# Depthwise convolution taps split between ScalarE and VectorE, and six adaLN jobs issued earlier, in a two-layer hybrid decoder trunk

## The chip, the cores and the metric

The kernel runs on one core of one Trainium2 chip. The metric is the device time of one execution in microseconds, as the median over runs. In this text PE is TensorE (PEld its weight loads), DVE is VectorE, ACT is ScalarE, POOL is GpSimd and SP is SyncE, whose queue issues the DMAs.

## What is computed

```python
D_MODEL, SEQ, DEPTH, D_FF = 2048, 256, 2, 5632
CONV_CH, CONV_WIDTH = 512, 31            # the depthwise convolution of this case
IN_COLS = SB_COLS + CONV_COLS + NSA_COLS + MLA_COLS   # 1536 + 1024 + 1304 + 672

def conformer_conv(u, dw_w, dw_b, ln_g, ln_b, pw_w, pw_b):
    a, g = jnp.split(u, 2, axis=-1)
    h = causal_dwconv(a * jax.nn.sigmoid(g), dw_w, dw_b)     # 31 taps per channel
    ...                                                       # LayerNorm over the channels
    return jax.nn.silu(h) @ pw_w + pw_b

def hybrid_mixer(h, w_in, ...):
    u = h @ w_in
    u_sb, u_conv, u_nsa, u_mla = jnp.split(u, [OFF_CONV, OFF_NSA, OFF_MLA], axis=-1)
    o_sb = stick_breaking_attention(...)   # 8 heads
    o_conv = conformer_conv(u_conv, ...)
    o_nsa = nsa_attention(...)             # compressed, selected and window branches
    o_mla = mla_attention(u_mla, ...)      # low-rank q and kv latents
    y = concat([o_sb, o_conv, o_nsa, o_mla])
    y = rms_norm(y.reshape(B, T, 4, 512), group_norm.reshape(4, 512))
    return y.reshape(B, T, 2048) @ w_o

def conv_glu_ffn(h, w_up, conv_w, conv_b, w_down):
    u = causal_dwconv(h @ w_up, conv_w, conv_b)               # 3 taps
    a, g = jnp.split(u, 2, axis=-1)
    return (jax.nn.silu(g) * a) @ w_down

def reference(x, c, ada_w, ada_b, ...):
    cond = jax.nn.silu(c)
    for l in range(DEPTH):
        mod = cond @ ada_w[l] + ada_b[l]                      # adaLN: 2048 x 12288 weights a layer
        sh1, sc1, g1, sh2, sc2, g2 = jnp.split(mod, 6)
        h = rms_norm(x, norm_mix[l]) * (1 + sc1) + sh1
        x = x + g1 * hybrid_mixer(h, ...)
        h = rms_norm(x, norm_ffn[l]) * (1 + sc2) + sh2
        x = x + g2 * conv_glu_ffn(h, ...)
    return x
```

## The kernel before

**Stages.** Each of the two layers has a mixing part (input projection, the four head groups MLA, NSA, stick-breaking and convolution, then w_o) and an FFN (w_up, activation, w_down). The 256 tokens lie along the free dimension for most tiles (128 channels by 256 tokens). All weights come once from HBM, in chunks of at most 128x1024 in fp32. `load_w` loads such a chunk into one of four buffers of the tag `raw`. For most matmuls it then makes two fp32r parts of it: ACT casts `hi` (L247), DVE subtracts to get `lo` (L249), each in a ring of three. With `whole=True`, as the input projection of layer 0 does, PE multiplies the fp32 chunk itself.

**Order.** Each engine runs its instructions in one fixed order, which a list scheduler writes out when the kernel is built, from priorities and data dependences. All loads go through SP's one queue, in that order too: a load whose buffer is not free yet holds up the loads behind it.

**adaLN jobs.** The modulation vectors of the gates and of the FFN are made on DVE. A job of `ada_jobs` loads two chunks `adaw` (512 KB each, ring of three, L163) and runs one dot product with the conditioning vector on each (L167). Layer 0 needs 16 jobs for the mixing gate, then 32 for the FFN's shift and scale, then 16 for its gate. `tick` issues jobs: each `load_w` adds `rate[0]` to a credit, and a whole credit issues a job. The dots of a job run at the next job, or right behind a `lo` (L249). `rate[0]` is 0 throughout layer 0's input projection, and is set by `phase` afterwards (table RATE). `mod` issues at once whatever is still missing when a vector is used. For layer 0's FFN, `norm_chunk` uses `mod` in that way.

**The input projection of layer 0** (`mix_in_behind`) loads wconv and wlq beside the adaLN chunks of the first norm, and then calls `nsa_kv`, which loads 16 chunks wnkv (412 KB) and runs 128 matmuls (L322) on them. In layer 1 `nsa_kv` comes later, behind the taps.

**The taps.** `conv_glu` writes the gated signal `ug` (128 x 4 x 286 with its left padding). `conv_taps` then makes for each of 31 taps and each of the four 128-channel tiles one DVE instruction on 128x256: the first tap as a TENSOR_SCALAR with the bias (L617), the other 30 as a SCALAR_TENSOR_TENSOR, times a per-channel weight plus `acc` (L621). That is 124 per layer. The weights lie in the tile `vec`, one DMA per layer, which holds all small vectors. The taps are written with a priority that is lowered by DW_LATE = 800, so that they fill gaps. `conv_ln` needs them all. It is written behind the MLA group and the first stick-breaking gemm (`sb_gemm(l, 0)`).

**Tag sq4.** Pool `mr` has one buffer of 128x1024 with the tag `sq4`. It serves in turn `cv` (the projection's copy), the scratch of the squares in `group_norm_n` (L522, here the norm of MLA's output `om`), a tile of the NSA group, and the scratch of `conv_ln` and of later norms.

Of the kernel before, what the change touches and what calls it, by code (L numbers as in the profile page):

```python
# [11 lines left out]
F32 = mybir.dt.float32  # L12
F32R = mybir.dt.float32r
BF16 = mybir.dt.bfloat16
AF = mybir.ActivationFunctionType
ALU = mybir.AluOpType
# [4 lines left out]
P = 128  # L21
T = 256
# [7 lines left out]
CW = 31  # L30
# [32 lines left out]
RATE = ((0.45, 0.9, 0.45), (0.2, 0.8, 0.45))  # L63

RATE_FFN = ((0.16, 0.36), (0.12, 0.12))
ADA_LATE = ((2500, 2500, 300, 1500, 1500), (2500, 1000, 300, 2500, 2500))
GATE = ((1, 0, 0, 1, 1), (1, 0, 0, 1, 1))
DW_LATE = 800
# [7 lines left out]
def tile_trunk(ctx: ExitStack, tc: tile.TileContext, io, out, L):  # L76
    nc = tc.nc
# [64 lines left out]
    def vec(l, name):  # L142
        o, w = VEC[name]
        if o >= NVEC:
            if (l, 1) not in vecs:
                vecs[l, 1] = cp.tile([P, NVECS], F32, name=f"vs{l}")
                nc.sync.dma_start(vecs[l, 1], io["vecs"][l])
            return vecs[l, 1][:, o - NVEC:o - NVEC + w]
        if (l, 0) not in vecs:
            vecs[l, 0] = cp.tile([P, NVEC], F32, tag="vec", name="vec", bufs=1)  # L150
            nc.sync.dma_start(vecs[l, 0], io["vec"][l])
        return vecs[l, 0][:, o:o + w]
# [19 lines left out]
    def ada_dot(l, s, j, raw):  # L172
        for hf in range(2):
            ada_mul(ada_load(l, s, j, hf), s, j, hf, raw)
# [43 lines left out]
    def phase(l, i):  # L218
# [3 lines left out]
        gate[0] = GATE[l][i]  # L222
        late[0] = ADA_LATE[l][i]

# [10 lines left out]
    rate = [0.0]  # L235
# [23 lines left out]
    def products(w, act, weights_stand):  # L259

        hi, lo = w
        if lo is None:
            return [(hi, act)]
        x, xl = act[:, 0, :], act[:, 1, :]
        return [(hi, x), (hi, xl), (lo, x)] if weights_stand else [(hi, x), (lo, x), (hi, xl)]
# [68 lines left out]
    def act_whole():  # L334
        return actp.tile([P, 4, T], F32, tag="act", name="actw", bufs=12)
# [12 lines left out]
    def norm_stats(x, sp, pp, tag):  # L348

        ss = pp.tile([P, 2, T], F32, tag=tag, name="ss")  # L350
        acc = sp.tile([P, 4, T], F32, name="nacc")
        for c in range(4):
            xc = x[:, 4 * c:4 * c + 4, :]
            if c == 0:
                nc.scalar.activation(acc, xc, AF.Square)
                continue
            sq = sp.tile([P, 4, T], F32, tag="nsq4", name="sq", bufs=2)
            nc.scalar.activation(sq, xc, AF.Square)
            nc.vector.tensor_add(acc, acc, sq)
        nc.vector.tensor_add(acc[:, 0:2, :], acc[:, 0:2, :], acc[:, 2:4, :])  # L360
        for c in range(2):
            nc.tensor.matmul(ss[:, 0, :], ones, acc[:, c, :], start=(c == 0), stop=(c == 1))
        r = sp.tile([P, T], F32, tag="nr", name="r", bufs=1)
        rsqrt(r, ss[:, 0, :], D)
        return r
# [25 lines left out]
    def norm_chunk(dst, xc, r, a, sh, sp):  # L391

        t1 = sp.tile([P, T], F32, tag="nsq", name="t1", bufs=2)
        nc.vector.scalar_tensor_tensor(t1, xc, a, r, op0=ALU.mult, op1=ALU.mult)
        if is_whole(dst):
            nc.scalar.activation(dst, t1, AF.Identity, bias=sh)  # L396
            return
        nc.scalar.activation(dst[:, 0, :], t1, AF.Identity, bias=sh)
        nc.vector.scalar_tensor_tensor(  # L399
            dst[:, 1, :], t1, sh, dst[:, 0, :].bitcast(F32), op0=ALU.add, op1=ALU.subtract  # L400
        )

    def norm_hs():
        hs = []
        for _ in range(KD // 2):
            ht = act_pair()
            hs += [ht[:, 0], ht[:, 1]]
        return hs
# [12 lines left out]
    def mm_n(outs, w, h, first, last):  # L421

        prods = products(w, h, False)
        for tt in range(2):
            for i, (ww, xx) in enumerate(prods):
                for o, c0, c1, f in outs(tt):
                    nc.tensor.matmul(
                        o, xx[:, tt * P:(tt + 1) * P], ww[:, c0:c1],
                        start=(first and i == 0 and f), stop=(last and i == len(prods) - 1),
                        skip_group_check=True,  # L430
                    )
# [19 lines left out]
    def mix_in_behind(l, x, sp, pp, mr, conv):  # L451

        r = norm_stats(x, sp, pp, "gp")
        a = cp.tile([P, KD], F32, tag="amul", name="amul", bufs=2)
        g, ab = vec(l, "norm_mix"), vec(l, "ada_b")
        sh = cp.tile([P, KD], F32, name="sh0")
        sc = cp.tile([P, KD], F32, name="sc0")
        raws = [cp.tile([P, 2, KD], F32, name=f"raw0_{i}") for i in range(2)]
        hs, hw = norm_hs(), []
        for _ in range(KD // 4):  # L460
            t = act_whole()
            hw += [t[:, i, :] for i in range(4)]
        ps = [pp.tile([P, 2, T], F32, tag="gp", name="gt") for _ in range(4)]
        px = [pp.tile([P, 2, T], F32, tag="gx", name="gt") for _ in range(4)]
        for k in range(KD):
            for s, m in ((1, sc), (0, sh)):
                if s == 0:
                    w = load_w(io["wconv"][l, k], True)
                ada_dot(l, s, k, raws[s])
                nc.vector.scalar_tensor_tensor(  # L470
                    m[:, k:k + 1], raws[s][:, 0, k:k + 1], ab[:, s * KD + k:s * KD + k + 1],
                    raws[s][:, 1, k:k + 1], op0=ALU.add, op1=ALU.add,
                )
            nc.vector.scalar_tensor_tensor(
                a[:, k:k + 1], sc[:, k:k + 1], 1.0, g[:, k:k + 1], op0=ALU.add, op1=ALU.mult
            )
            norm_chunk(hw[k], x[:, k, :], r, a[:, k:k + 1], sh[:, k:k + 1], sp)
            split_chunk(hs[k], hw[k])
            mm_t(px, w, hw[k], 8, k == 0, k == KD - 1)
            if k == KD - 1:  # L480
                cv = [mr.tile([P, 4, T], F32, tag=t, name="cv") for t in ("sq4", "acc")]
                cv = [t[:, 2 * i:2 * i + 2, :] for t in cv for i in range(2)]
                for i in range(4):
                    nc.scalar.copy(cv[i], px[i])
                conv(cv)
            w = load_w(io["wlq"][l, k], True)
            mm_t(ps, w, hw[k], 5, k == 0, k == KD - 1)
            mm_n(lambda tt: [(ps[3][:, tt, :], 640, 896, tt == 0)], w, hw[k], k == 0, k == KD - 1)
        return hs, ps, nsa_kv(l, hw, mr, pp, "gx")

    def split_chunk(dst, src):
# [115 lines left out]
        return ug  # L607

    def conv_taps(l, ug, mp):
        acc = mp.tile([P, 4, T], F32, tag="acc", name="acc")  # L610
        dw = vec(l, "dw_w")
        db = vec(l, "dw_b")
        for j in range(CW - 1, -1, -1):
            for c in range(4):
                w = dw[:, c * CW + j:c * CW + j + 1]
                if j == CW - 1:
                    nc.vector.tensor_scalar(  # L617
                        acc[:, c, :], ug[:, c, j:j + T], w, db[:, c:c + 1], op0=ALU.mult, op1=ALU.add
                    )
                else:  # L620
                    nc.vector.scalar_tensor_tensor(  # L621
                        acc[:, c, :], ug[:, c, j:j + T], w, acc[:, c, :], op0=ALU.mult, op1=ALU.add
                    )
                yield acc

    def conv_ln(l, acc, mp, pp):
# [163 lines left out]
    def nsa_kv(l, h, mp, pp, tag="gp"):  # L790
        nkv = mp.tile([P, 2, 824], F32, name="nkv")
        ps = [[pp.tile([P, 2, T], F32, tag=tag, name="pn").rearrange("p a b -> p (a b)")[:, 0:412]
               for _ in range(2)] for _ in range(2)]
        gemm_n([io["wnkv"][l, k] for k in range(KD)], h, 824,
               lambda tt: [(ps[tt][s], s * 412, s * 412 + 412, True) for s in range(2)])
        for tt in range(2):
            for s in range(2):
                nc.scalar.copy(nkv[:, tt, s * 412:s * 412 + 412], ps[tt][s])
        return nkv
# [250 lines left out]
    for l in range(L):  # L1050
# [7 lines left out]
        with ExitStack() as s1:  # L1058
            p8 = _Tagged(pool(s1, f"p8_{l}", space=PSUM), {"gp": 4, "gx": 4})
            with ExitStack() as s0:  # L1060
                ug = []
# [5 lines left out]
                if l:  # L1067
                    h, ps = mix_in(l, x, r, sp, p8, conv)
                else:
                    h, ps, nkv = mix_in_behind(l, x, sp, p8, mr, conv)  # L1070
# [41 lines left out]
        for mg in range(2):  # L1112
            ps = gemm_t(pp, [io["wo"][l, mg, k] for k in range(KD)], y, 8)
            for m in range(8):
                c = mg * 8 + m
# [10 lines left out]
        with ExitStack() as s2:  # L1126
# [3 lines left out]
            h = norm_hs()  # L1130
# [10 lines left out]
            def up(g):  # L1141
                rate[0] = RATE_FFN[l][0] if g else 0.0
                ps = [pp.tile([P, 2, T], F32, tag="gp", name="gt") for _ in range(4)]
# [26 lines left out]
            def down(k0, acts, st=None):  # L1170
                rate[0] = RATE_FFN[l][1]
                for mg in range(4):
# [179 lines left out]
```

## Time and profile before

| | |
|---|---|
| median of 3 runs | 2453.43 us (2445.65 to 2476.61) |
| the profiled execution, its own time | 2452.41 us |
| span of that execution in the trace | 2450.6 us |
| PE busy | 2369.3 us (97%) |
| DVE busy | 1937.6 us (79%) |
| ACT busy | 1225.8 us (50%) |
| DMA moved | 609.82 MB, 249 GB/s over the span |

The span runs from the first to the last instruction in the trace, and the profiled execution is 1.8 us longer than it. A busy share is an average over stages with different limits, so the rows below are taken by stage. In layer 0, 165 to 209 us is `nsa_kv`. From 209 to 314 us run MLA, the first stick-breaking gemm and the preparation of NSA, up to the first use of the NSA scores (L951). The rest of the mixing part and w_o run from 314 us to 535 us, and the FFN begins there. In layer 1 the stretch from 1341 to 1471 us holds `nsa_kv`, the taps and MLA.

### The profile page before, as it was taken

What the parts mean: (1) busy time and instruction counts of PE and PEld (TensorE: products, weight loads), DVE (VectorE), ACT (ScalarE), POOL (GpSimd) and SP (SyncE); (2) the same over time, 40 slices, a digit from 0 to 9 for tenths busy, and PEclk for the clock granted to TensorE, in tenths of its full rate; (3) what the DMA queues carried; (4) which work ended last, traced back from release to release, by engine and by line L of the source; (5) the groups of instructions that cost most, each with busy time, mean ns of one, the idle gap of its engine ahead of it and who ended that gap; (6) DMA issues with size and microseconds to landing.
All of it is one profiled execution on the core that took longest, in us unless ns stands there. A gap on an engine that the chain in (4) does not pass through costs nothing.

```text
span 2450.6 us, 38162 instructions
## 1 busy us (share of the span) xinstructions
PE 2369.3 (97%) x14496; PEld 2100.5 (86%) x14496; DVE 1937.6 (79%) x3212; ACT 1225.8 (50%) x1880; POOL 25.2 (1%) x40
## 2 busy tenths in 40 slices
PE   7788999989999999999999999999999999999999
PEld 5666999978888888888879999998888888888887
DVE  6679988888888887888876999888887765566755
ACT  2124666446555534556335476554655553355543
POOL 0000000000000000000001000000000000000000
PEclk9999999999999999999999999999999999999999
DMA  9975787987777898778885567898667655556654
GB/s 326 328 275 183 246 270 270 336 290 255 256 255 248 297 320 293 260 240 270 288 295 168 187 218 244 269 321 317 236 231 241 224 191 191 189 186 196 190 190 164
DMA packets 169098, 609.82 MB, mean 249 GB/s; under 512 B 19025, under 2 KB 20945, under 8 KB 168401
## 3 DMA queue, kind: packets, MB, share of 16 engines
q1 hardware_dynamic: 168914, 607.39, 73.0%
q8 instruction: 113, 1.85, 0.3%
q14 instruction: 71, 0.58, 0.1%
HBM read 603.12 MB, written 4.19 MB: 248 GB/s over the span
## 4 chain that ended last, share of the span: by engine, by line
PE 84%; DMA 6%; DVE 6%; ACT 3%; issue 1%; SPq 0%; DVEq 0%; ACTq 0%
PE gt L300 39%; PE gt L304 20%; PE gt L279 9%; DMA adaw<-in_ada_dram 6%; PE gt L415 3%; PE pn L322 3%; DVE adaw L167 2%; PE po L591 1%; DVE lo L249 1%; PE pv L322 1%; PE pq L322 1%; PE s L565 1%; PE tp L586 1%; PE ss L382 1%; ACT hi L247 1%
## 5 line engine op out<-in xcount | busy, mean ns | idle before, releaser
L247 ACT CAST hi<-raw 128x1024 fp32r<-128x1024 f32 (+3 forms) x716 | 741.9, 1037 | 852.9 <-PE gt L300 602.2
L249 DVE TENSOR_TENSOR lo<-raw,hi 128x1024 fp32r<-128x1024 f32 (+3 forms) x716 | 859.7, 1204 | 358.0 <-ACT hi L247 356.3
L300 PE MATMUL gt<-act,hi 128*128 128x512 f32 x2816 | 983.7, 395 | 10.8 <-DVE act L399 7.8
L304 PE MATMUL gt<-act,lo 128*128 128x256 f32 x2816 | 786.6, 280 | 4.0 <-DVE lo L249 4.0
L300 PEld LDWEIGHTS gt<-act,hi 128*128 128x128 f32 x2816 | 530.9, 189 | 133.0 <-DVE act L399 8.6
L304 PEld LDWEIGHTS gt<-act,lo 128*128 128x128 f32 x2816 | 533.4, 190 | 5.3 <-DVE lo L249 5.3
L167 DVE SCALAR_TENSOR_TENSOR adaw<-adaw,cond 128x1024 f32<-128x1024 f32 x384 | 465.3, 1220 | 69.9 <-DMA adaw<-in_ada_dram 68.6
L300 PE MATMUL gt<-g,hi 128*128 128x512 f32 x1408 | 490.5, 394 | 0.2 <-DVE x L1179 0.2
L304 PE MATMUL gt<-g,lo 128*128 128x256 f32 x1408 | 393.0, 279 | 0.0
L300 PEld LDWEIGHTS gt<-g,hi 128*128 128x128 f32 x1408 | 264.4, 188 | 60.3 <-issue 0.4
L279 PE MATMUL gt<-act,hi 128*128 128x256 f32 x1600 | 303.2, 287 | 0.0
L304 PEld LDWEIGHTS gt<-g,lo 128*128 128x128 f32 x1408 | 265.7, 189 | 0.3
L279 PEld LDWEIGHTS gt<-act,hi 128*128 128x128 f32 x1600 | 251.4, 191 | 1.4
L279 PE MATMUL gt<-act,lo 128*128 128x256 f32 x800 | 230.7, 288 | 1.5 <-DVE lo L249 1.5
L279 PEld LDWEIGHTS gt<-act,lo 128*128 128x128 f32 x800 | 153.1, 191 | 2.5 <-DVE lo L249 2.3
L415 PE MATMUL gt<-actw,raw 128*128 128x256 f32 x416 | 105.7, 417 | 26.7 <-ACT actw L396 26.7
L415 PEld LDWEIGHTS gt<-actw,raw 128*128 128x128 f32 x416 | 86.1, 210 | 46.1 <-ACT actw L396 32.6
L1155 ACT ACTIVATE u<-v,vec 128x256 f32<-128x256 f32 x176 | 96.7, 597 | 10.2 <-DVE v L1152 5.3
L621 DVE SCALAR_TENSOR_TENSOR acc<-ug,vec,acc 128x256 f32<-128x256 f32 x240 | 99.1, 478 | 0.0
L1156 DVE SCALAR_TENSOR_TENSOR u<-v,vec,u 128x255 f32<-128x255 f32 x176 | 80.1, 479 | 11.9 <-ACT u L1155 11.9
L1151 ACT COPY v<-gt 128x256 f32<-128x256 f32 x176 | 63.5, 369 | 47.5 <-PE gt L304 34.2
L1159 DVE SCALAR_TENSOR_TENSOR u<-v,vec,u 128x254 f32<-128x254 f32 x176 | 80.1, 479 | 2.6
(290 smaller groups left out, 2152.6 us busy)
## 6 DMA issues: line engine op xcount, KB each, us to landing
adaw<-in_ada_dram SPq DMA_DIRECT2D x384, 512.0 KB, 5.5
raw<-in_wup_dram SPq DMA_DIRECT2D x352, 512.0 KB, 4.3
raw<-in_wdn_dram SPq DMA_DIRECT2D x176, 512.0 KB, 4.4
raw<-in_wo_dram SPq DMA_DIRECT2D x64, 512.0 KB, 5.2
raw<-in_wconv_dram SPq DMA_DIRECT2D x32, 512.0 KB, 4.3
raw<-in_wsqk_dram SPq DMA_DIRECT2D x32, 512.0 KB, 4.3
raw<-in_wlq_dram SPq DMA_DIRECT2D x32, 448.0 KB, 4.8
raw<-in_wnkv_dram SPq DMA_DIRECT2D x32, 412.0 KB, 3.4
```

The lines of the kernel that those rows point to most:

```text
L167: nc.vector.scalar_tensor_tensor(w, w, 1.0, cond[:, hf * 1024:hf * 1024 + 1024], op0=ALU.mult, op1=ALU.mult, accum_out=raw[:, hf, j:j + 1],)
L247: nc.scalar.copy(hi[:, :n], raw[:, :n])
L249: sub = nc.vector.tensor_sub(lo[:, :n], raw[:, :n], hi[:, :n].bitcast(F32))
L279: nc.tensor.matmul(ps[m // 2][:, m % 2, :], ww[:, c], x, start=(k == 0 and i == 0 and m % 2 == 0), stop=(k == K - 1 and i == len(prods) - ...
L300: nc.tensor.matmul(banks[m].rearrange("p a t -> p (a t)"), hi[:, c], x2, start=(k == 0), stop=False, skip_group_check=True,)
L304: nc.tensor.matmul(banks[m][:, 1, :], lo[:, c], acts[k][:, 0, :], start=False, stop=(k == K - 1), skip_group_check=True,)
L322: nc.tensor.matmul(o, x[:, tt * P:(tt + 1) * P], ww[:, kk * N + c0:kk * N + c1], start=(k == 0 and i == 0 and first), stop=(k == K - 1 and ...
L415: nc.tensor.matmul(ps[m // 2][:, m % 2, :], ww[:, m * P:(m + 1) * P], xx, start=(first and i == 0 and m % 2 == 0), stop=(last and i == len ...
L621: nc.vector.scalar_tensor_tensor(acc[:, c, :], ug[:, c, j:j + T], w, acc[:, c, :], op0=ALU.mult, op1=ALU.add)
L1155: nc.scalar.activation(u[:, q, :], v, AF.Identity, scale=w2, bias=fb[:, i:i + 1])
L1156: nc.vector.scalar_tensor_tensor(u[:, q, 1:], v[:, :T - 1], w1, u[:, q, 1:], op0=ALU.mult, op1=ALU.add)
L1159: nc.vector.scalar_tensor_tensor(u[:, q, 2:], v[:, :T - 2], w0, u[:, q, 2:], op0=ALU.mult, op1=ALU.add)
```

## The change

It does two things.

1. `conv_taps`: for the 30 later taps ScalarE multiplies (`Copy` with the per-channel weight as its scale, 128x256 each, L627 in the changed kernel) into a new tile `pr`, and DVE adds two channel tiles at once (TENSOR_TENSOR on 128x512, L630). Per layer that is 120 instructions on ACT and 60 on DVE in place of 120 on DVE. The first tap stays as it was (L623). `pr` takes the tag `sq4`, so it has its turn in that one buffer, between `cv` and the scratch of `group_norm_n` (L525).
2. `rate[0] = RATE_KV = 0.4` ahead of layer 0's `nsa_kv`: its 16 loads give 6.4 credits, so six jobs (12 chunks `adaw`) are issued among them. The rate after them is that of the table, as before.

```diff
--- before.py
+++ after.py
@@ -63,6 +63,8 @@
 RATE = ((0.45, 0.9, 0.45), (0.2, 0.8, 0.45))
 
 RATE_FFN = ((0.16, 0.36), (0.12, 0.12))
+
+RATE_KV = 0.4
 ADA_LATE = ((2500, 2500, 300, 1500, 1500), (2500, 1000, 300, 2500, 2500))
 GATE = ((1, 0, 0, 1, 1), (1, 0, 0, 1, 1))
 DW_LATE = 800
@@ -486,6 +488,7 @@
             w = load_w(io["wlq"][l, k], True)
             mm_t(ps, w, hw[k], 5, k == 0, k == KD - 1)
             mm_n(lambda tt: [(ps[3][:, tt, :], 640, 896, tt == 0)], w, hw[k], k == 0, k == KD - 1)
+        rate[0] = RATE_KV
         return hs, ps, nsa_kv(l, hw, mr, pp, "gx")
 
     def split_chunk(dst, src):
@@ -607,20 +610,24 @@
         return ug
 
     def conv_taps(l, ug, mp):
+
         acc = mp.tile([P, 4, T], F32, tag="acc", name="acc")
         dw = vec(l, "dw_w")
         db = vec(l, "dw_b")
+        pr = mp.tile([P, 4, T], F32, tag="sq4", name="pr")
         for j in range(CW - 1, -1, -1):
-            for c in range(4):
-                w = dw[:, c * CW + j:c * CW + j + 1]
-                if j == CW - 1:
-                    nc.vector.tensor_scalar(
-                        acc[:, c, :], ug[:, c, j:j + T], w, db[:, c:c + 1], op0=ALU.mult, op1=ALU.add
-                    )
-                else:
-                    nc.vector.scalar_tensor_tensor(
-                        acc[:, c, :], ug[:, c, j:j + T], w, acc[:, c, :], op0=ALU.mult, op1=ALU.add
-                    )
+            for p in range(2):
+                for c in (2 * p, 2 * p + 1):
+                    w = dw[:, c * CW + j:c * CW + j + 1]
+                    if j == CW - 1:
+                        nc.vector.tensor_scalar(
+                            acc[:, c, :], ug[:, c, j:j + T], w, db[:, c:c + 1], op0=ALU.mult, op1=ALU.add
+                        )
+                    else:
+                        nc.scalar.activation(pr[:, c, :], ug[:, c, j:j + T], AF.Copy, scale=w)
+                if j < CW - 1:
+                    h = slice(2 * p, 2 * p + 2)
+                    nc.vector.tensor_add(acc[:, h, :], acc[:, h, :], pr[:, h, :])
                 yield acc
 
     def conv_ln(l, acc, mp, pp):
```

The scheduler puts the instructions in another order. Line numbers of the changed kernel are larger than before by 2 to 7.

**SP, loads of `nsa_kv` in layer 0.** `con`, `gains` and `vec` are the constants, the gains of the rotary tables and the small vectors, `wuq` is MLA's first weight. Before:

```order
L242 DMA raw<-in_wlq_dram 128x896
L242 DMA raw<-in_wnkv_dram 128x824 x2
L102 DMA con<-in_con_dram 128x1054
L663 DMA gains<-in_gains_dram 128x768
L151 DMA vec<-in_vec_dram 128x513
L242 DMA raw<-in_wnkv_dram 128x824
L147 DMA vs_8029<-in_vecs_dram 128x128
L242 DMA raw<-in_wnkv_dram 128x824 x13
L104 DMA msk<-in_msk_dram 128x256
L242 DMA raw<-in_wuq_dram 128x384 x3
```

and with the change, the last third of the same loads:

```order
L244 DMA raw<-in_wnkv_dram 128x824 x2
L165 DMA adaw<-in_ada_dram 128x1024
L244 DMA raw<-in_wnkv_dram 128x824
L104 DMA con<-in_con_dram 128x1054
L244 DMA raw<-in_wnkv_dram 128x824
L670 DMA gains<-in_gains_dram 128x768
L153 DMA vec<-in_vec_dram 128x513
L244 DMA raw<-in_wnkv_dram 128x824
L149 DMA vs_7924<-in_vecs_dram 128x128
L244 DMA raw<-in_wnkv_dram 128x824
L106 DMA msk<-in_msk_dram 128x256
L244 DMA raw<-in_wuq_dram 128x384 x2
```

The load of `vec` moved from behind the second of the 16 wnkv loads to behind the 14th; ahead of these rows stand the second to tenth wnkv loads with adaw loads between them.

**DVE, the first taps of layer 0** (`ug` is their input, L167 or L169 the adaLN dots). Before:

```order
L105 CAST identb<-con 128x128
L551 SCALAR_TENSOR_TENSOR e<-cv,e 128x512
L606 TENSOR_TENSOR ug<-cv,e 128x2x256
L551 SCALAR_TENSOR_TENSOR e<-cv,e 128x512
L617 TENSOR_SCALAR acc<-ug,vec 128x256 x2
L621 SCALAR_TENSOR_TENSOR acc<-ug,vec,acc 128x256 x2
L606 TENSOR_TENSOR ug<-cv,e 128x2x256
L621 SCALAR_TENSOR_TENSOR acc<-ug,vec,acc 128x256
L617 TENSOR_SCALAR acc<-ug,vec 128x256 x2
L621 SCALAR_TENSOR_TENSOR acc<-ug,vec,acc 128x256 x86
```

and with the change:

```order
L609 TENSOR_TENSOR ug<-cv,e 128x2x256
L554 SCALAR_TENSOR_TENSOR e<-cv,e 128x512
L169 SCALAR_TENSOR_TENSOR adaw,modr_2_831<-adaw,cond 128x1024
L609 TENSOR_TENSOR ug<-cv,e 128x2x256
L169 SCALAR_TENSOR_TENSOR adaw,modr_2_831<-adaw,cond 128x1024 x4
L185 TENSOR_TENSOR mod_2_832<-modr_2_831 128x4
L186 TENSOR_TENSOR mod_2_832<-mod_2_832,vs_140 128x4
L169 SCALAR_TENSOR_TENSOR adaw,modr_2_831<-adaw,cond 128x1024 x2
L107 CAST identb<-con 128x128
L623 TENSOR_SCALAR acc<-ug,vec 128x256 x4
L630 TENSOR_TENSOR acc<-acc,pr 128x512 x6
L108 CAST cmask<-msk 128x128
L109 CAST smask<-msk 128x128
```

Dots of the six jobs now stand ahead of the first tap (L617 before, L623 with the change), and where 86 taps stood in a row there are six adds.

**ACT, the norm of MLA's output in layer 0** (`sq,ss<-om` is that norm, the hi casts beside it are those of `sb_gemm(0, 0)`). Before:

```order
L815 ACTIVATE nksq<-nkv 128x384
L588 COPY pT<-tp 128x512
L815 ACTIVATE nksq<-nkv 128x384
L247 CAST hi<-raw 128x1024
L522 ACTIVATE sq,ss<-om 128x512
L247 CAST hi<-raw 128x1024
L522 ACTIVATE sq,ss<-om 128x512
L342 ACTIVATE ss<-ss,scal 128x2
L344 ACTIVATE ss<-ss 128x2
L247 CAST hi<-raw 128x1024
L539 ACTIVATE act<-tp,vec 128x256 x2
```

and with the change:

```order
L249 CAST hi<-raw 128x1024
L627 ACTIVATE pr<-ug,vec 128x256 x4
L249 CAST hi<-raw 128x1024
L627 ACTIVATE pr<-ug,vec 128x256 x4
L249 CAST hi<-raw 128x1024
L627 ACTIVATE pr<-ug,vec 128x256 x6
L249 CAST hi<-raw 128x1024
L627 ACTIVATE pr<-ug,vec 128x256 x18
L525 ACTIVATE sq,ss<-om 128x512 x2
L344 ACTIVATE ss<-ss,scal 128x2
L346 ACTIVATE ss<-ss 128x2
L542 ACTIVATE act<-tp,vec 128x256 x3
```

The norm moved from amid the casts of the gemm to behind the last of them and behind the last tap. On PE the transposes of `om` moved with it behind the last matmul of `sb_gemm(0, 0)`.

## Rows read from the trace of the kernel before

**Rows 1.** The page: busy times, and the chain of waits by engine

```profile
PE 2369.3 (97%) x14496; PEld 2100.5 (86%) x14496; DVE 1937.6 (79%) x3212; ACT 1225.8 (50%) x1880; POOL 25.2 (1%) x40
...
PE 84%; DMA 6%; DVE 6%; ACT 3%; issue 1%; SPq 0%; DVEq 0%; ACTq 0%
```

**Rows 2.** Windows: us; busy us (instructions) of PE, PEld, DVE, ACT, POOL; PEclk; DMA; GB/s

```profile
165.00:209.00 44.00, 44.00 (x129) 24.21 (x128) 43.27 (x107) 4.48 (x10) 3.90 (x6) 1.00 0.45 141
209.00:313.00 104.00, 95.41 (x705) 86.07 (x704) 96.65 (x191) 66.11 (x147) 5.38 (x8) 0.95 0.72 240
313.00:441.00 128.00, 127.27 (x958) 119.37 (x959) 111.38 (x222) 84.50 (x185) 0.31 (x1) 1.00 0.80 273
441.00:505.00 64.00, 64.00 (x529) 63.79 (x528) 52.80 (x81) 26.01 (x28) 0.00 (x0) 1.00 0.91 334
...
1341.00:1471.00 130.00, 128.95 (x896) 122.54 (x895) 126.91 (x256) 77.27 (x154) 5.37 (x8) 1.00 0.62 203
```

**Rows 3.** Timeline of the nsa_kv stage, SP, PE and DVE: start us, us, instruction, count

```profile
157.85 0.42 SPq L151 DMA_DIRECT2D vec<-in_vec_dram  x1
165.11 33.53 SPq L242 DMA_DIRECT2D raw<-in_wnkv_dram  x13
...
164.91 44.43 PE L322 MATMUL pn<-raw,actw 128*128 128x412 f32 x128
...
171.73 34.13 DVE L621 SCALAR_TENSOR_TENSOR acc<-ug,vec,acc 128x256 f32<-128x256 f32 x86
```

**Rows 4.** The tile vec: its first use by a tap, its time to landing

```profile
L617 DVE TENSOR_SCALAR acc<-ug,vec x4: 401/402/570, 168.5 to 171.4; 128x256 f32<-128x256 f32 x4
...
DMA to landing us min/median/max: 6.9/6.9/6.9
```

**Rows 5.** Timeline of DVE and ACT after 208 us: prices, and ends of idle times

```profile
208.52 1.05 ACT L247 CAST hi<-raw 128x384 fp32r<-128x384 f32 x2 [39.11 <-DMA raw<-in_wuq_dram]
...
248.66 0.68 DVE L767 TENSOR_TENSOR mk<-mk,rk 128x512 f32<-128x512 f32 x1
249.26 0.19 DVE L597 RECIPROCAL rs<-rs 128x8 f32<-128x8 f32 x1
...
252.41 1.22 DVE L167 SCALAR_TENSOR_TENSOR adaw<-adaw,cond 128x1024 f32<-128x1024 f32 x1
253.55 1.22 DVE L167 SCALAR_TENSOR_TENSOR adaw<-adaw,cond 128x1024 f32<-128x1024 f32 x1
...
275.36 0.88 DVE L527 TENSOR_SCALAR om<-om,ss 128x512 f32<-128x512 f32 x2
...
314.37 0.28 DVE L951 TENSOR_TENSOR cs<-sc,scl 128x120 f32<-128x120 f32 x1 [0.85 <-PE sc L946]
```

**Rows 6.** ACT instructions with per-channel operands: groups by form, and two in a row

```profile
L1155 ACT ACTIVATE u<-v,vec 128x256 f32<-128x256 f32 x176 | 96.7, 597 | 10.2 <-DVE v L1152 5.3
L398 ACT ACTIVATE act<-t,mod 128x256 fp32r<-128x256 f32 x48 | 21.8, 501 | 15.9 <-DVE t L394 11.3 <-DVE mod L184 4.6
...
527.85 0.91 ACT L398 ACTIVATE act<-t,mod 128x256 fp32r<-128x256 f32 x2
```

**Rows 7.** Start of layer 0's FFN: SP's timeline; windows of line L300 alone (PE, PEld)

```profile
536.18 9.92 SPq L163 DMA_DIRECT2D adaw<-in_ada_dram  x6
...
535.00:560.00 25.00, 15.73 (x40) 8.39 (x40) 0.86 0.86 301
560.00:585.00 25.00, 25.00 (x73) 13.50 (x73) 1.00 0.73 245
```

## The prediction

> **What bounds the kernel now.** The page comes first: PE is busy 97% of the span, and the chain that ended last lies 84% on PE, 6% each on DMA and DVE [rows 1]. So time taken off DVE is worth something only where PE waits for DVE, and time given to DVE or ACT costs nothing while PE has work. Averages hide where that is, so I read windows by stage next [rows 2]. From 165 to 209 us, layer 0's `nsa_kv`, PE works all 44.00 us and the DMA moves only 141 GB/s. The reader should see who else works there: DVE 43.27 us and ACT 4.48. DVE's time is the taps, 86 in a row in 34.13 us [rows 3]. They lie wholly beside PE's 44.43 us of L322 and so cost nothing. From 209 to 313 us it is different: DVE is busy 96.65 of 104 us, PE 95.41, ACT 66.11 [rows 2]. PE and DVE have almost the same load there, and what is added to DVE has 7.4 us of idle time to go into. From 313 to 505 us PE hardly pauses. In layer 1, 1341 to 1471 us, PE is busy 128.95 and DVE 126.91 of 130 us, and ACT 77.27 [rows 2].
>
> **When the taps can start.** The taps, old and new, read their weights from `vec`. Before, `vec` is issued at 157.85 us [rows 3], lands 6.9 us later, and the first tap runs at 168.5 us [rows 4]. With the change SP issues `vec` behind the 14th wnkv load. There are four `raw` buffers, so that load waits until PE is through the tenth chunk. PE takes 44.43/16 = 2.78 us a chunk and starts at 164.9 [rows 3], so that is 164.9 + 10 × 2.78 = 192.7 us. Add 6.9 us: the taps start at about 200 us instead of 168.5. The six jobs add 12 × 0.52 MB = 6.3 MB to 44 us, or 143 GB/s on top of 141. Their sum of 284 is below the 334 GB/s of a busy stretch [rows 2], so I take nothing for the stage itself. Its upper bound is 4 us. But 31 us in which taps were free are lost: only 20 ACT taps and ten adds stand ahead of the next load's cast, which stood at 208.5 us before [rows 5]; 50 of the 60 adds stand behind it.
>
> **Prices.** An old tap in a row is 34.13/86 = 0.397 us [rows 3]. An add on 128x512 is 0.68 us alone; in a row it starts the next after 249.26 − 248.66 = 0.60 us [rows 5]. Two old taps are 0.794, so DVE saves 0.19 us a pair, 60 × 0.19 = 11.6 us a layer. A dot in a row costs 253.55 − 252.41 = 1.14 us [rows 5]; I take 1.15. For the tap on ACT no row has Copy with a pointer as its scale. The nearest is L398, 128x256 with one per-channel operand: 0.501 us on average, and two take 0.91 us, so 0.455 in a row. L1155 with two such operands, 0.597, is the upper end; 0.41 my lower one, half of 0.91 less a tenth [rows 6]. 120 of them are 49 to 60 us a layer on ACT (72 at the very top).
>
> **209 us to the NSA scores, layer 0.** DVE gets 50 adds, 50 × 0.60 = +30.0 us, and loses the 23 old taps that ran after 209 us before, 23 × 0.397 = −9.1. Twelve more dots stand ahead of the scores, since jobs that are no longer behind now ripen here: 12 × 1.15 = +13.8. That is +34.6 us on an engine with 7.4 us idle. At best it is therefore +27. What makes it worse is the norm of MLA's output. Its square shares the buffer `sq4` with `pr` and so waits for the last add. It now stands behind the gemm's last cast and 18 more ACT taps, 18 × 0.455 = 8.2 us. From that norm to the scores the kernel before took 314.37 − 275.36 = 39 us [rows 5], under gemm matmuls that have all been used up now. The DVE work of that stretch, 12 dots and some 20 us of small steps, is in the sum already. The waits between PE, ACT and DVE in it are not: 0 to 15 us, and I take 7. So **+42 us** at the scores, with ends of +27 and +50.
>
> ACT has 66.11 + 100 × 0.455 = 112 us there, under DVE's 131, so I don't let it set the end.
>
> **313 to 505 us.** The twelve dots that ran early are missing later, and PE has some slack to close up: 958 matmuls at the pace of the next window, 64/529 us each [rows 2], would take 116 of the 128 us. At most 12 us come back. Only a third of it is likely, since the shapes differ and PE is busy 127.27 us: **−4 us**.
>
> **Start of layer 0's FFN.** Before, three jobs were still missing: 8 × 0.45 + 30 × 0.9 + 32 × 0.45 = 45 credits from the loads up to there against 48 jobs. Their six chunks took SP 9.92 us to issue at 536.18 us, and L300 had only 40 matmuls in 25 us where the next 25 us have 73 [rows 7]. PE's granted clock fell to 0.86 as well, that is, part of the time at the lower of its two levels, after waits of PE. (73 − 40)/73 × 25 = 11.3 us are lost there. With 6.4 more credits nothing is missing: **−11 us**, with ends of 0 (the queue behind them is also full) and −11.3.
>
> **Layer 1.** Here `vec` comes early and the taps lie beside `nsa_kv` as before. ACT gets 54.6 us: 77.3 + 54.6 = 132 of 130. DVE saves 11.6 and gets ten more dots ahead of the norm, 11.5: nothing. Three engines are now all full in one window, the norm waits for the last tap, and I take **+4 us**, between 0 and +12.
>
> **Sum.** 42 − 4 − 11 + 4 = +31 us. The profiled execution took 2452.41 us, which is 1 us below the median of 2453.43, so the forecast is 2483.4 against it, and 2484 against the median. 2% is 49 us, about what a measurement of this kernel can tell from no change.
>
> One page of the Trainium skill speaks against the change itself. "ScalarE: Activation LUTs", section "Rules for kernel authors", says to use VectorE rather than ScalarE for multiplies and adds, up to about three times faster per element in bf16. The rows here are fp32 and show 0.397 us against 0.455, which isn't three. The same page, section "What ACT_TABLE_LOAD costs", gives 186 ns + 0.833 ns an element, 93 ns for each pointer operand and an overlap of 93 ns; an estimate from it is 0.399 us for a tap in a row, and the sum would not change by it, since ACT stays under DVE's load.
>
> **Rivals.**
> *The time is given back* (chance 0.17). The dots only fill gaps, the waits of the norm are covered, and DVE's 7.4 us of idle time is used: 30.0 − 9.1 − 7.4 = +13.5 at the scores. All 12 us come back before 505, the 11 at the FFN too, layer 1 is unchanged: 2453 + 13.5 − 12 − 11 = about 2443. For it speaks that dots stand in the order as fillers; against it, that twelve of them stand by name ahead of the scores' first DVE step.
> *The two engines take turns* (chance 0.22), which ends on the other side. Both engines have a fixed order, and each add stands behind other work on DVE, each pair of taps behind other work on ACT. A buffer half of `pr` is free for the next pair only when its add is done. If taps and add don't overlap, a pair costs 2 × 0.49 + 0.68 = 1.66 us instead of the 0.60 in my sum, 50 × 1.06 = +53 more: 2484 + 53 = 2537. It passes 2% when a pair costs over 0.60 + 18/50 = 0.96 us. Against it speaks that `pr` has two halves, so one pair can be multiplied while the other is added.
> *A multiply on ACT costs three times one on DVE* (chance 0.03): 3 × 0.397 = 1.2 us a tap. ACT then has 66 + 100 × 1.2 = 186 us where there are 104, +82 at the scores; in layer 1 77 + 144 = 221 where there are 130, +91; 2453 + 82 − 4 − 11 + 91 = 2611. L398 at 0.501 speaks against it [rows 6]. It is what the skill's rule just named would make of this kernel at its full factor.
> *The jobs don't change the FFN's start:* the 11 us stay lost, 2495. That lies inside the forecast's own range.
>
> **How the numbers follow.** The forecast of 2484 has 0.58, with its own range of 2460 to 2505 (from +27 − 12 − 11 + 0 to +50 + 0 − 0 + 4, a little narrower since the ends don't meet). For 8 in 10 the range reaches down to the case that gives back, and up into the first half of the turns: 2440 to 2525. Outside lie about half of the turns, the three-fold price and a little below. Slower by over 2% (2502): most of the turns, the three-fold price and a twentieth of the forecast, 0.27. Faster by over 2% (2404): no case gives it, 0.01. Within 2%: 0.72.
>
> **What would show it.** `vec` issued near 193 us and the first tap near 200. DVE largely idle before that, but for ten or so dots. ACT's taps at 0.41 to 0.50 us, adds at 0.60 to 0.68. The first NSA scores at about 356 us instead of 314, with PE idle between the last gemm matmul and them. No gap in L300 and a full clock at the start of layer 0's FFN. ACT nearly full in layer 1's window, which is a few us longer. I would be wrong if PE were idle only briefly ahead of the scores, if taps and adds alternated, or if PE lost its higher clock level in the new idle stretch for long, which would lengthen what follows.

## The result, and the profile after

The changed kernel takes 2498.18 us (median of 6 runs, 2477.95 to 2499.61), the kernel before 2451.4 us (6 runs, 2443.46 to 2476.61). The ratio is 1.0148, with a 95% interval of 1.0109 to 1.0187, so it is 27 to 46 us slower. A second measurement of both on one chip gave 1.0123 (1.0084 to 1.0162). The profiled execution of the changed kernel took 2498.75 us with a span of 2496.5, which is 45.9 us longer than the span before.

The page of the changed kernel, busy times and the chain by engine [rows 1]:

```profile
PE 2389.3 (96%) x14496; PEld 2107.0 (84%) x14496; DVE 1920.8 (77%) x3092; ACT 1317.9 (53%) x2120; POOL 24.9 (1%) x40
...
PE 80%; DMA 7%; DVE 6%; ACT 5%; issue 2%; SPq 0%; DVEq 0%; ACTq 0%
```

DVE lost 17 us of work and ACT gained 92. The time went up all the same, and 4% of the chain moved away from PE. The windows of layer 0's mixing part in the changed kernel show where [rows 2]:

```profile
165.00:209.00 44.00, 42.87 (x125) 23.37 (x123) 22.52 (x40) 12.36 (x30) 5.54 (x8) 1.00 0.79 278
209.00:313.00 104.00, 84.89 (x596) 77.37 (x596) 97.61 (x171) 91.69 (x211) 5.37 (x8) 0.88 0.69 226
313.00:360.00 47.00, 28.00 (x173) 23.84 (x174) 41.10 (x94) 18.74 (x53) 0.31 (x1) 0.67 0.60 200
```

Beside `nsa_kv` DVE works 22.52 us where it worked 43.27. From 209 to 313 us it is as full as before (97.61 us, before 96.65), but with more work still to come, and from 313 to 360 us PE is busy 28 of 47 us at a granted clock of 0.67, that is, most of the time at the lower of its two levels. The trail leads to the timelines of SP, DVE and ACT of the changed kernel around the first taps [rows 3, 4]:

```profile
191.72 0.42 SPq L153 DMA_DIRECT2D vec<-in_vec_dram  x1
...
196.95 3.01 DVE L623 TENSOR_SCALAR acc<-ug,vec 128x256 f32<-128x256 f32 x4 [4.02 <-DMA vec<-in_vec_dram]
...
197.03 1.71 ACT L627 ACTIVATE pr<-ug,vec 128x256 f32<-128x256 f32 x4 [29.35 <-DMA vec<-in_vec_dram]
201.00 6.71 ACT L627 ACTIVATE pr<-ug,vec 128x256 f32<-128x256 f32 x16 [2.26 <-DVE acc L630]
```

`vec` is issued at 191.72 us instead of 157.85, and ACT sat idle 29.35 us until it had landed. The end of the taps, in the timelines of ACT, DVE and PE of the changed kernel:

```profile
311.91 1.71 ACT L627 ACTIVATE pr<-ug,vec 128x256 f32<-128x256 f32 x4 [0.64 <-DVE acc L630]
314.26 0.91 ACT L627 ACTIVATE pr<-ug,vec 128x256 f32<-128x256 f32 x2 [0.64 <-DVE acc L630]
316.61 0.63 ACT L525 ACTIVATE sq<-om 128x512 f32<-128x512 f32 x1 [1.44 <-DVE acc L630]
...
312.40 1.21 DVE L169 SCALAR_TENSOR_TENSOR adaw<-adaw,cond 128x1024 f32<-128x1024 f32 x1
...
313.55 1.28 DVE L630 TENSOR_TENSOR acc<-acc,pr 128x512 f32<-128x512 f32 x2
...
319.82 1.21 PE L538 MATMUL tp<-con,om 128*128 128x128 f32 x4 [16.56 <-DVE om L530]
```

The norm of MLA's output (L525) begins when the last add is done, at 316.61 us. PE had finished the gemm, and had no work for 16.56 us until the transposes behind that norm could run. The scores of the changed kernel, in the view of the tile `cs` [rows 5 has 314.37]:

```profile
L958 DVE TENSOR_TENSOR cs<-sc,scl x4: 275/280/282, 353.5 to 1592.8; 128x120 f32<-128x120 f32 x4
```

They come at 353.5 us, 39.1 us late.

At the start of layer 0's FFN the stall has gone. L302 (L300 before) in two windows of 25 us from the first activation of the FFN's norm on, first the changed kernel, then the kernel before [rows 7]:

```profile
556.00:581.00 25.00, 23.92 (x68) 12.78 (x68) 1.00 0.49 168
581.00:606.00 25.00, 25.00 (x72) 13.32 (x71) 1.00 0.73 247
...
518.00:543.00 25.00, 22.14 (x55) 11.81 (x55) 0.84 0.80 268
543.00:568.00 25.00, 17.95 (x48) 9.65 (x48) 0.90 0.77 271
```

The 50 us hold 140 matmuls with the change and 103 before; 37 at 72 in 25 us are 12.8 us.

Not all of the rest belongs to the change. In the FFNs PE is busy without a pause at full granted clock in both kernels, yet it doesn't run equally fast. PE alone, two stretches of the FFNs of layer 0 and layer 1, first the changed kernel, then the kernel before:

```profile
640.00:740.00 100.00, 100.00 (x568) 1.00 0.73 245
2050.00:2200.00 150.00, 150.00 (x851) 1.00 0.58 186
...
640.00:740.00 100.00, 100.00 (x578) 1.00 0.73 250
2050.00:2200.00 150.00, 150.00 (x868) 1.00 0.59 190
```

A matmul comes every 173 ns in the kernel before and every 176 in the changed one. That made 12.6 us between the 21st and the last load of w_up in layer 0, and 13.0 us from the 21st load of w_up in layer 1 to the end. Kernels 7 and 8 below show that this belongs to an execution and not to the kernel. Without it the two profiles are 45.9 − 25.6 = 20 us apart; the second profile of the changed kernel, in the same way, 26 us. Against the second profile of the kernel before the two are 24 and 30 us.

### The profile page after: what moved, and what is told of

Its sections match the earlier page's. It is cut to its first block, busy times and chain, and to the rows that moved or that the text cites. A ratio compares the mean times of both kernels' runs of the same rounds, so it can differ in the third digit from the quotient of the medians.

```text
span 2496.5 us, 38363 instructions
## 1 busy us (share of the span) xinstructions
PE 2389.3 (96%) x14496; PEld 2107.0 (84%) x14496; DVE 1920.8 (77%) x3092; ACT 1317.9 (53%) x2120; POOL 24.9 (1%) x40
## 4 chain that ended last, share of the span: by engine, by line
PE 80%; DMA 7%; DVE 6%; ACT 5%; issue 2%; SPq 0%; DVEq 0%; ACTq 0%
PE gt L302 39%; PE gt L306 20%; PE gt L281 8%; DMA adaw<-in_ada_dram 6%; DVE adaw L169 3%; PE gt L417 2%; ACT pr L627 1%; PE po L594 1%; DVE lo L251 1%; PE s L568 1%; PE pq L324 1%; PE pn L324 1%; ACT hi L249 1%; PE pv L324 1%; DVE acc L630 1%
## 5 line engine op out<-in xcount | busy, mean ns | idle before, releaser
L302 PE MATMUL gt<-act,hi 128*128 128x512 f32 x2816 | 996.8, 399 | 6.9 <-DVE act L401 6.9
L302 PEld LDWEIGHTS gt<-act,hi 128*128 128x128 f32 x2816 | 529.8, 188 | 140.0 <-DVE act L401 7.7
L169 DVE SCALAR_TENSOR_TENSOR adaw<-adaw,cond 128x1024 f32<-128x1024 f32 x384 | 465.2, 1219 | 79.0 <-DMA adaw<-in_ada_dram 78.1
L302 PE MATMUL gt<-g,hi 128*128 128x512 f32 x1408 | 498.3, 399 | 0.0
L302 PEld LDWEIGHTS gt<-g,hi 128*128 128x128 f32 x1408 | 265.1, 188 | 64.9
L627 ACT ACTIVATE pr<-ug,vec 128x256 f32<-128x256 f32 x240 | 106.0, 500 | 35.6 <-DMA vec<-in_vec_dram 29.4
L1163 DVE SCALAR_TENSOR_TENSOR u<-v,vec,u 128x255 f32<-128x255 f32 x176 | 80.3, 478 | 12.8 <-ACT u L1162 12.8
```

The lines of the kernel that those rows point to most:

```text
L169: nc.vector.scalar_tensor_tensor(w, w, 1.0, cond[:, hf * 1024:hf * 1024 + 1024], op0=ALU.mult, op1=ALU.mult, accum_out=raw[:, hf, j:j + 1],)
L302: nc.tensor.matmul(banks[m].rearrange("p a t -> p (a t)"), hi[:, c], x2, start=(k == 0), stop=False, skip_group_check=True,)
L627: nc.scalar.activation(pr[:, c, :], ug[:, c, j:j + T], AF.Copy, scale=w)
L1163: nc.vector.scalar_tensor_tensor(u[:, q, 1:], v[:, :T - 1], w1, u[:, q, 1:], op0=ALU.mult, op1=ALU.add)
```

## The experiments

All times are compared with the kernel before, measured beside each run on the same chip. Marks used for the profiles: the scores (L951 before, 314.4 us), the first activation of layer 0's FFN norm (L398 before, 516.6), and the issue of the 21st load of w_up (574.0).

**1. Taps alone.** The changed kernel without the line of the rate:

```diff
-        rate[0] = RATE_KV
```

> The changed kernel without the earlier adaLN jobs (rate 0 in nsa_kv of layer 0, as before): taps on ScalarE and DVE alone. vec then stands behind the second wnkv load again, and 94 of the 120 ScalarE taps stand ahead of the first wuq cast. My theory (the queue position of vec and what follows from it costs the time): scores of layer 0 within 5 us of 314, the stall at the start of layer 0's FFN is back, the whole within 5 us of the kernel before (2451, so 2446 to 2456). Rival (multiplying on ScalarE costs the time, by taking turns or by its price): scores 20 us or more late, the whole near 2475 or above.

Measured: ratio 1.002 (0.9986 to 1.0054). `vec` is issued at 154.5 us. From the views of the tiles `acc` and `cs`, first tap and scores:

```profile
L622 DVE TENSOR_SCALAR acc<-ug,vec x4: 407/412/414, 168.3 to 170.4; 128x256 f32<-128x256 f32 x4
...
L957 DVE TENSOR_TENSOR cs<-sc,scl x4: 279/282/283, 315.1 to 1558.6; 128x120 f32<-128x120 f32 x4
```

So 240 multiplies on ScalarE, and 17 us less work on DVE (1920.2 us on its page), change the time by no more than the interval leaves, −3 to +13 us. The rival that ScalarE's price or its turns with DVE cost the time, 20 us or more at the scores, has fallen.

**2. Jobs alone.** The kernel before with the rate:

```diff
+RATE_KV = 0.4
...
+        rate[0] = RATE_KV
         return hs, ps, nsa_kv(l, hw, mr, pp, "gx")
```

> The kernel before with the earlier adaLN jobs alone; taps all on DVE. vec stands behind the 14th wnkv load. My theory: first tap near 197 us; 89 more taps after 209 us ahead of the scores, 89 x 0.397 = 35 us on DVE, less 11 dots that now run later, 13 us: scores 20 to 25 us late, 12 us of it given back at the start of the FFN, the whole about 2460. Rival (ScalarE's multiplying costs the time): scores at 314, 12 us gained at the FFN, the whole about 2440.

Measured: ratio 1.0158 (1.0107 to 1.0208), as slow as the changed kernel. `vec` is issued at 192.6 us and the first tap runs at 198.1, as expected. But the scores come at 314.1 us, not 20 late, and the 21st load of w_up is 42.0 us late. Windows of that kernel, 209 to 313 us and the start of the FFN:

```profile
209.00:313.00 104.00, 93.57 (x696) 85.15 (x697) 95.33 (x209) 65.85 (x148) 5.39 (x8) 0.93 0.39 134
...
528.00:572.00 44.00, 23.22 (x100) 18.75 (x100) 36.74 (x71) 10.75 (x16) 0.00 (x0) 0.73 0.82 272
572.00:620.00 48.00, 39.70 (x180) 32.22 (x180) 40.50 (x72) 19.66 (x30) 0.00 (x0) 0.82 0.86 284
```

DVE has the same load as before in the first window, and the DMA only 134 GB/s instead of 240. The scheduler had put the taps where 21 dots stood, and the dots later: none is left in that window. Their bill came at the FFN's start, where 41 dots stand between 500 and 620 us (26 before) and L301 on PE waits 21.7 us for what DVE makes behind them. That the lost DVE time would be paid was right. The place was not, and nor was the size: I expected a whole of about 2460 us, and the kernel is 1.6%, 39 us, above the one before.

**3. vec early.** The changed kernel with one line ahead of the rate:

```diff
+        vec(l, "dw_w")
         rate[0] = RATE_KV
```

> The changed kernel, with vec loaded ahead of nsa_kv's first load; both parts of the change stay. 77 ScalarE taps stand ahead of the first wuq cast. My theory: first tap near 168 us, 22 adds after 209 us (13 us) in place of 23 old taps (9 us), as many dots as before: scores 0 to 8 us late, PE idle for less than 10 us ahead of them, 12 us gained at the FFN: the whole 2440 to 2448, which is 50 us below the changed kernel. Rival (ScalarE's multiplying): still 2475 or above.

Measured: ratio 0.9999 (0.9968 to 1.0029). The scores come at 317.2 us, and PE is busy from 303 to 353 us, where the changed kernel had 21.26 us:

```profile
303.00:353.00 50.00, 49.98 (x399) 47.67 (x398) 45.44 (x92) 31.70 (x71) 0.31 (x1) 1.00 0.68 229
```

One line takes the whole loss away, with all adds and all jobs in place. It isn't the other small loads that were pushed with `vec`: `con` and `gains` stay late here, issued at 186.96 and 189.76 us. The gain that I expected beside it is smaller: from the FFN's norm to the 21st load of w_up 10 us are gained, but the norm comes 5 us late, so that this load is 5.5 us early in this profile, and the interval leaves room for 8 us at most.

**4. Own scratch.** The changed kernel, with the squares of `group_norm_n` in a buffer of their own:

```diff
-            sq = mp.tile([P, 4, T], F32, tag="sq4", name="sq")
-            nc.scalar.activation(
-                sq.rearrange("p a b -> p (a b)")[:, :512], o[:, tt, :], AF.Square, accum_out=ss[:, tt:tt + 1]
-            )
+            sq = mp.tile([P, 2 * T], F32, tag="gsq", name="sq", bufs=1)
+            nc.scalar.activation(sq, o[:, tt, :], AF.Square, accum_out=ss[:, tt:tt + 1])
```

> The changed kernel, with a buffer of its own for the squares of group_norm_n, so that the norm of MLA's output doesn't wait for the taps; vec is late as in the changed kernel. The norm stands amid the gemm's casts again, and 59 taps behind it. If the coupling by the buffer (steps of the NSA preparation without matmuls beside them) is a large part: scores 15 to 25 us earlier than in the changed kernel, whole about 2480. If DVE's load after 209 us (30 us of adds and 9 of dots) sets the time: scores 0 to 9 us earlier, whole 2490 to 2498.

Measured: ratio 1.0166 (1.0135 to 1.0197). Scores at 344.5 us, 9 us earlier than in the changed kernel (12 against its second profile) and still 30 late. That is as much as DVE has more work, in the window from 209 us to the scores:

```profile
209.00:344.00 135.00, 100.75 (x717) 90.44 (x718) 127.31 (x236) 105.11 (x247) 5.38 (x8) 0.84 0.69 219
```

DVE is busy 127.31 us where before it was 97.16 up to 314 us, and idle 7.7 us against 7.8. So the buffer shared with `pr` costs some 10 us at the scores, and DVE's load fits the other 30. In the time of the whole these 10 us don't show: at the first norm of layer 1 this profile is still 6 us ahead of the changed kernel's, but the mixing part of layer 1, which the edit touches too, then takes 5.6 us longer.

**5. vec late by hand.** Kernel 1 (taps alone, no jobs) with the load of `vec` put behind the last wnkv load:

```diff
-        return hs, ps, nsa_kv(l, hw, mr, pp, "gx")
+        nkv = nsa_kv(l, hw, mr, pp, "gx")
+        with tc.issue_after(last_load[0].ins):
+            vec(l, "dw_w")
+        return hs, ps, nkv
```

> Taps on ScalarE and DVE, without the earlier adaLN jobs, and with vec's load put behind the last wnkv load by hand. If the place of vec in SP's queue is the cause by itself: first tap near 203 us, the norm of MLA's output behind the gemm's last cast again, scores 35 to 45 us late, the stall at the FFN's start there as before, the whole 30 to 45 us above the run of taps alone (about 2495 to 2505). If the extra jobs are (their transfers and their dots): scores less than 10 us late, the whole near 2465.

Measured: ratio 1.0185 (1.0127 to 1.0243). `vec` issued at 195.6 us. First tap and scores (tiles `acc`, `cs`), and L302 in the first 25 us from the FFN norm on:

```profile
L625 DVE TENSOR_SCALAR acc<-ug,vec x4: 408/408/413, 199.4 to 200.3; 128x256 f32<-128x256 f32 x4
...
L960 DVE TENSOR_TENSOR cs<-sc,scl x4: 277/280/283, 356.0 to 1605.9; 128x120 f32<-128x120 f32 x4
...
559.00:584.00 25.00, 16.46 (x40) 9.03 (x41) 0.80 0.69 215
```

The place of one 128x513 load in SP's queue costs 41.6 us at the scores, 40.9 against kernel 1, without any earlier job. `con` and `gains` are early here, issued at 150.82 and 151.35 us. And without the jobs the FFN's start stalls: 40 matmuls, against 68 in the changed kernel. The two effects of the change are apart now.

**6. Jobs with vec early, taps on DVE.** Kernel 2 with `vec(l, "dw_w")` ahead of the rate, as in kernel 3.

> The kernel before with the earlier jobs and with vec ahead of nsa_kv's first load; taps all on DVE. Against the run with vec early and both parts this tells what the taps on ScalarE bring. If only what runs in free time matters: 77 taps ahead of the first wuq cast, 47 behind it, 24 x 0.397 = 10 us more on DVE than before, scores 0 to 10 us late, 15 us or more gained at the FFN's start, the whole within 6 us of the run with vec early. If DVE's 11.6 us a layer matter: 15 to 25 us above it.

Measured: ratio 1.0033 (0.9998 to 1.0067), 0.3% above kernel 3. Scores at 315.2 us. Some 18 us are lost in w_o, where the put-off dots come due. SP's timeline there:

```profile
474.48 7.39 SPq L164 DMA_DIRECT2D adaw<-in_ada_dram  x4
481.96 0.38 SPq L243 DMA_DIRECT2D raw<-in_wo_dram  x1
483.82 5.35 SPq L164 DMA_DIRECT2D adaw<-in_ada_dram  x3
489.27 0.38 SPq L243 DMA_DIRECT2D raw<-in_wo_dram  x1
```

Each load of w_o waits for three or four adaw loads, which wait for dots. Kernel 3 came out ahead by some 8 us, between the two expectations (within 6, or 15 and more). The two intervals overlap and come from different chips, so this tells neither; whether the split helps where six jobs run early is open.

**7 and 8. Both kernels once more**, unchanged, for the pace of the FFNs.

> The changed kernel once more. In the first profiles the matmuls of both FFNs came every 176.6 ns with the change and every 173.4 ns without, and in the experiments sometimes one, sometimes the other. If that pace belongs to the execution and not to the kernel: at least one FFN of this profile may be at 173.4, and the times spread over 2475 to 2500. If the kernel sets it: both at 176.6 again. The scores at 353 us in either case.

> The kernel before once more, for its pace in the FFNs: both at 173.4 ns a matmul if the kernel sets it, else one or both at 176.6; scores at 314 us, the stall at the FFN's start as before.

Measured: the changed kernel has a ratio of 1.0123, scores at 356.5 us and a span of 2484.1; the kernel before has 314.1 and 2459.7. PE alone, the same two stretches, first the changed kernel:

```profile
640.00:740.00 100.00, 100.00 (x567) 1.00 0.73 242
2050.00:2200.00 150.00, 150.00 (x867) 1.00 0.61 189
```

and the kernel before:

```profile
640.00:740.00 100.00, 100.00 (x579) 1.00 0.77 252
2050.00:2200.00 150.00, 150.00 (x851) 1.00 0.60 186
```

Both kernels have FFNs of either pace. It belongs to the execution.

**9 and 10. Half the rate, vec early**, with the taps split (kernel 3) and all on DVE (kernel 6):

```diff
-RATE_KV = 0.4
+RATE_KV = 0.2
```

> Both parts, vec ahead of nsa_kv, and half the rate there (0.2: 3.2 credits, just the three jobs that were missing). 89 ScalarE taps stand ahead of the first wuq cast. If the gain at the FFN's start needs only the missing jobs: scores 0 to 4 us late, 10 us gained up to the 20th w_up load, with its other stages as before; 5 to 12 us below the kernel before at equal pace of the FFNs, a ratio of 0.996 or less. If it is the DMA load there that sets the stall, not the jobs: the stall is back, ratio 1.000.

> The same with the taps all on DVE as before: 94 of 124 taps ahead of the first wuq lo, against 101 before. If ScalarE's part of the taps brings nothing where DVE's time beside nsa_kv is free: within 5 us of the other run of this call at equal pace. If DVE's 11.6 us a layer count: 8 to 20 us above it.

Measured: 1.0023 (0.9993 to 1.0054) and 1.0021 (0.9992 to 1.0051). In the first the scores come 9.9 us late and the 21st load of w_up 0.9 early: what the FFN's start gained, the scores had lost. In the second they come 0.6 late and 1.7 early. From the FFN's norm to the 21st load kernel 9 gained the 10 us that I expected, so the three missing jobs are enough for that gain; but neither beats the kernel before, the ratio of 0.996 was not reached, and the split makes no difference between the two.

## Why the prediction was right, point by point

- **vec and the first tap**: forecast near 193 and 200 us, measured 191.72 and 196.95 (195.2 and 201.2 in the second profile). Kernels 3 and 5 show that this one load is the cause: moved ahead, the loss is gone, though `con` and `gains` stay late; moved back alone, it is there, though they are early.
- **+42 at the scores**: +39 and +42. DVE worked 132.47 us from 209 to 353 us against 97.16 from 209 to 314, so +35 for a forecast of +34.6, and was idle 11.5 us against 7.8, so +4 for the 7 that I took for waits. So the load is right in size, but one reason in it was wrong. The dots ahead of the scores, 33 between the first wuq `lo` and the scores where the kernel before has 21, don't need the earlier jobs: kernel 5 has none, and 35 stand there. Kernel 2 has the jobs and no dot there. How many stand there is the scheduler's choice, and on the chain from 209 us to the scores they hold some 7 us, against 2 before. Whether they delay the scores or fill a stretch that is long for another reason was not tried, so that the sum of DVE's work fits to a microsecond is in part luck. The sum also had no term for PE's clock, whose loss I had named only as a sign of being wrong. It was lost: from 303 to 353 us the granted clock is 0.62, that is, the lower level for some 38 of the 50 us. It fell within PE's wait of 16.56 us. On the chain the same 32 matmuls, first before at the higher level, then in the changed kernel, cost 3.0 us more:

```profile
296.54 3.64 PE pc L870 x32
...
341.03 6.64 PE pc L877 x32
```

- **−11 at the FFN's start**: −13 in both profiles of the changed kernel, between the first activation of the FFN's norm and the 21st load of w_up. About 3 to 5 of that also come without the jobs (kernels 5 and 1), so the jobs bring about 9.
- **−4 up to 505 us and +4 in layer 1**: −1 and +3 from the scores up to the FFN's norm; −3 and −4 from layer 1's first norm to its FFN's norm. Both are mis-sized by some 3 to 8 us, in opposite directions, and these errors largely cancel in the sum, which is luck. In layer 1, 1376 to 1506 us, ACT is busy 118.90 us, where I had put 132, and PE 126.80 of 130.
- **The price on ACT**: 16 taps in 6.71 us, 0.42 us in a row, in the lower part of the 0.41 to 0.50 that I allowed. The Trainium skill, "ScalarE: Activation LUTs", section "What ACT_TABLE_LOAD costs", led to an estimate of 0.399; the trace nearly agrees. The rival of a three-fold price had no ground.
- **Taking turns**: in the last stretch, 307 to 316 us, four taps come every 2.35 us, since a dot stands between two adds: a pair costs 1.18 us there. But ACT waited for adds 6.0 us in all, in 9 places in both layers, so it didn't decide.
- **Sum**: +31 forecast, 36 by the ratio (27 to 46), 30 in the second measurement; 20 to 30 us between the profiles once the FFNs' pace is taken out. So the forecast lies at the upper end of the last, and it stays open whether some of the difference in the medians is that pace too: the runs of the two kernels spread over 22 and 33 us. The upper end of the range, 2505, takes layer 1 with +4 although its own end was +12; with that it would have been 2515.

Why does ScalarE's part of the taps bring nothing? The Trainium skill, "Perfetto Trace Analysis", section "Optimizing Scalar/DVE Operations", says that moving work from DVE to ScalarE may make sense where DVE is saturated. On average it isn't, and beside `nsa_kv`, where the taps lay, its 43 us were free as long as PE had 44 us of matmuls. Kernels 1 and 10 agree; kernel 6 leaves open whether the split helps where more dots come due.

## What to carry to other kernels

An extra load is not only its bytes: in a queue that issues in order, and under a scheduler that fills it, it can push a small load that much else waits for. So look in the new order for what was pushed, not only for what was added. Work that lies free beside another engine costs nothing only while it can start in time; when it starts late its whole price comes due, and the scheduler may put it off to a place (scores, w_o, the FFN's start) far from the cause. And ahead of reading a difference between two profiles, compare a stretch that the change cannot touch.

## What the runs showed of the hardware that I had not expected

- A stream of matmuls with PE always busy and the granted clock at 1.00 runs at either of two paces, a matmul about every 173 or every 176 ns (100 us by 579 matmuls, by 567). Both kernels' FFNs had either, and one execution had both (kernel 8: 173 in layer 0, 176 in layer 1). The difference is some 13 us an FFN. What decides it is open.
- DVE and GpSimd slowed each other where they ran side by side. The first taps of the changed kernel took 0.68 to 0.94 us each on DVE, against 0.41 in kernel 5. At the same time GpSimd works on the rotary tables, which had waited for a pushed load too (`gains`); in kernel 5 it had finished at 161.6 us. Over all profiles, 30 of layer 0's first taps ran beside no GpSimd instruction and took 0.40 to 0.41 us; of the 18 that overlapped one, 17 took 0.57 to 0.94. The rows of GpSimd in the changed kernel, and rows of GpSimd and DVE in kernel 10:

```profile
196.33 1.41 POOL L684 TENSOR_TENSOR Cn<-gains,con 128x256 f32<-128x256 f32 x2 [195.40 <-DMA gains<-in_gains_dram]
197.69 1.52 POOL L684 TENSOR_TENSOR Sn<-gains,con 128x256 f32<-128x256 f32 x2
199.17 1.24 POOL L684 TENSOR_TENSOR Cm<-gains,con 128x192 f32<-128x192 f32 x2
...
180.22 25.57 POOL L680 TENSOR_TENSOR Cn<-gains,con 128x256 f32<-128x256 f32 x2 [179.29 <-DMA gains<-in_gains_dram]
...
178.65 25.42 DVE L624 SCALAR_TENSOR_TENSOR acc<-ug,vec,acc 128x256 f32<-128x256 f32 x64
...
204.26 5.93 DVE L624 SCALAR_TENSOR_TENSOR acc<-ug,vec,acc 128x256 f32<-128x256 f32 x8
```

It is some 2 us of DVE's time in the changed kernel. In kernel 10 it goes the other way: 64 taps run in a row at 0.40 us, and GpSimd takes 25.57 us for two instructions that take 1.41 in the changed kernel. Only when that row has ended does it go on, and the next eight taps take 5.93 us together. The spans of GpSimd are rough in these profiles, and no run was made for this alone.
